# A two-layer hybrid block: Hyena filters stored without their norm, and another order of the start

## The chip, the cores and the metric

The kernel runs on one core of a Trainium2 chip. The metric is the device time of one execution in microseconds (us). The core has five engines with a queue of instructions each: TensorE (PE, with the loading of weights shown apart as PEld), VectorE (DVE), ScalarE (ACT), GpSimd (POOL) and SyncE (SP). Most DMAs of this kernel are issued by SP.

## The reference, cut to what matters

Two layers; in each, a modulated RMS norm feeds one input projection shared by four mixers (a gated recurrence, differential attention, a convolution module and Hyena), then an output projection and a mixture-of-experts FFN. 1024 latent tokens run in both layers, 256 context tokens in the first alone. The shift and scale of the norms are the modulation, `silu(c) @ w_ada + b_ada`, once for `c` and once for `c_ctx`. The change concerns the modulation and the filters of Hyena:

```python
def hyena_filters(L, w_f1, b_f1, freq, w_f2, b_f2, w_f3, decay):
    ...
    f = jnp.sin(freq * (feats @ w_f1 + b_f1))
    f = jnp.sin(freq * (f @ w_f2 + b_f2))
    h = (f @ w_f3) * jnp.exp(-t_unit[:, None] * jnp.abs(decay))
    h = h.astype(jnp.float32).reshape(L, HYENA_ORDER, 2, W_D)
    energy = jnp.sum(jnp.square(h[:, :, 0]), 0) + jnp.sum(jnp.square(h[1:, :, 1]), 0)
    return h * lax.rsqrt(energy + EPS)[None, :, None, :]
...
def hyena_mixer(pd, filt, conv_w, conv_b, h_bias):
    u = dwconv(pd, conv_w, conv_b, (HYENA_SHORT // 2, HYENA_SHORT // 2))
    v, x1, x2 = jnp.split(u, HYENA_ORDER + 1, -1)
    z = v
    for o, gate in enumerate((x1, x2)):
        z = gate * long_conv_bidir(z, filt[:, o, 0], filt[:, o, 1], h_bias[o])
    return z
```

`long_conv_bidir` is a convolution through Fourier transforms plus `z * bias`. There are three sets of filters, none of which depends on `x`: 1024 taps for the first layer's latent tokens, 256 taps for its context tokens, and 1024 taps for the second layer's latent tokens. Since each gate is multiplied into the result of its filter, channel by channel, a factor of a filter may as well stand in its gate.

## The kernel before, in words

**The three filters.** `run` makes them by three calls of `filters`, whose parts are called by number: 0 is the first layer's long filter, 1 the short one for the context, 2 the second layer's long one. A filter has three steps. *network* (letter `p`) loads its weights and computes two sine layers; the argument of each sine is reduced on DVE in a row of small instructions, the sine itself is on ACT; its result is the tile `fc`. *order* (letter `h`, here called the decays) makes, for each block of 128 positions and each of the two gates, a matmul of `fc` with `w3`, an exponential window `e` on ACT, their product on DVE into `hl` (long) or `hs` (short), its square on ACT, and the sum of squares `acc` on POOL: 16 such windows in a long filter, 4 in the short one. Then come the energy by a matmul with ones (L1615), a square root (L1618), the sum and the difference of the filter's two directions (L1620, L1621), the skip bias put into the first tap, and the reciprocal `rs`. *transform* (letter `d`) makes the Fourier transform as matmuls of tables `tab` (128x1024 each, from DRAM) with butterflies of the filter on DVE and POOL (`f_x`, `f_y`, `f_d`; the short filter goes in without them). Each result of 128x512 is multiplied by `rs` on its way out of PSUM (L1651) and stored to DRAM (`hd`, `hdc`), for the convolutions much later. A long transform has 57 such matmuls in two halves and one for the last frequency, 58 in all; the short one has 10.

**The modulation.** `modulation` (letter `m`) streams `w_ada` through three buffers named `wada`, each load 128x4x256 (512 KB), and multiplies it with `sT`, the Silu of the two vectors: four matmuls per load into four row groups of one PSUM tile `mp`. A group of 16 loads gives 2048 columns; the first layer's groups 0 to 2 are made at the start, the others later. At a group's end four small additions put the bias `bada` on, and four stores write `modd` to DRAM.

**The start.** A list, START, names the order in which `run` writes these steps; `n` stands for the loading of the first layer's parameters (L920), of which four rows are of `modd`, and the first norm with its transposes (L1036), after which the input projection begins (L1065):

```python
START = "p0 p1 p2 h0 m0012 h1 d1 h2 d0 n d2"
```

The framework that builds the kernel takes the steps in that order of preference, and may put an instruction ahead of others where its inputs are expected earlier; what it decides is fixed, and each engine then runs its instructions in that order. A DMA stands in the queue of SP among the others. PSUM tiles of the filters' matmuls are five (`mm`), tables have five buffers, `ht` two.

**The gates.** In each layer `hyena_in` (L1713 on) runs Hyena's short convolution on six blocks of 128 channels: 0 and 1 are `v`, 2 to 5 the two gates. One multiplication with the bias on POOL and two multiply-adds on DVE (L1730) cover latent and context tokens together (1281 columns in the first layer, 1024 in the second).

## Time and profile before

| | |
|---|---|
| time, median of 3 runs | 3575.4 us (3574.82 to 3578.94) |
| time of the profiled execution | 3583.19 us |
| its span in the trace | 3581.3 us |
| mean granted TensorE clock | 0.923 of full speed |
| busy share of PE, PEld, DVE, ACT, POOL | 86%, 58%, 64%, 44%, 20% |

The span is the time between the first and the last instruction of the profiled execution; its own time is 1.9 us longer. The busy shares are means over the whole program; the change touches above all the first 277 us of it, so the stretches of that part say more.

### The profile page before, as it was taken

Reading aid. Unit: us, or ns where it says so; the run is one execution under the profiler, and the core shown is the slowest. Engines: PE = TensorE matmul, PEld = TensorE weight load, DVE = VectorE, ACT = ScalarE, POOL = GpSimd, SP = SyncE. Lnnn points to the kernel's source line nnn. Section 1 sums busy time; section 2 is a strip of 40 time slices with the busy share of each in tenths; the row PEclk is TensorE's granted clock in tenths of the full one; section 3 lists DMA queues with packets and bytes.
Section 4 is the critical chain, followed back from the end, with each engine's and each line's share of the span. In section 5 each row is a group of like instructions: output and inputs, shape, how many; then the busy total and the mean of one; then the engine's idle time right before and its main releaser. Section 6 shows DMA issues by size and latency. Waiting matters only on the chain. (4 is left out here: it accounts for less than half of the span.)

```text
span 3581.3 us, 43827 instructions
## 1 busy us (share of the span) xinstructions
PE 3073.7 (86%) x14952; PEld 2071.0 (58%) x14952; DVE 2274.8 (64%) x3297; ACT 1564.7 (44%) x2537; POOL 722.5 (20%) x579
## 2 busy tenths in 40 slices
PE   5798888997899699999997587799779799899993
PEld 1246665775678354676554465667657655465551
DVE  6674885787768433476543778588876653355626
ACT  4234334772334233455543444377323343344533
POOL 2212451003210111111110435300330111111102
PEclk8899899998999699999999798899899899999996
DMA  5752226215565888987878512311546489988796
GB/s 185 230 192 61 69 90 212 70 39 191 161 210 174 286 305 307 369 292 258 318 254 322 170 40 92 135 57 46 174 145 230 151 287 379 378 283 285 270 349 236
DMA packets 415375, 743.33 MB, mean 208 GB/s; under 512 B 46219, under 2 KB 181240, under 8 KB 415146
## 3 DMA queue, kind: packets, MB, share of 16 engines
q1 hardware_dynamic: 397546, 702.69, 56.6%
q0 software_dynamic: 17600, 37.79, 3.1%
q8 instruction: 119, 1.95, 0.2%
q14 instruction: 110, 0.90, 0.1%
HBM read 656.13 MB, written 105.30 MB: 213 GB/s over the span
## 5 line engine op out<-in xcount | busy, mean ns | idle before, releaser
L679 DVE TENSOR_TENSOR wl<-wr,wh 128x1024 fp32r<-128x1024 f32 (+1 forms) x440 | 516.2, 1203 | 395.8 <-ACT wh L678 382.8
L678 ACT ACTIVATE wh<-wr 128x1024 fp32r<-128x1024 f32 (+1 forms) x440 | 442.1, 1038 | 331.5 <-PE mm L730 192.6
L734 PE MATMUL mm<-wr,xl 128*64 128x512 f32 x1216 | 327.6, 607 | 3.4 <-DVE xl L690 1.6
L1065 PE MATMUL mm<-hh,wih 128*128 128x512 f32 (+1 forms) x752 | 290.6, 387 | 13.8 <-ACT stg L1129 8.3
L1065 PE MATMUL mm<-hh,wil 128*128 128x512 f32 (+1 forms) x752 | 289.4, 386 | 10.5 <-POOL wil L951 9.7
L730 PE MATMUL mm<-wh,xh 128*128 128x512 f32 x704 | 288.7, 411 | 6.8 <-ACT wh L678 6.2
L1065 PE MATMUL mm<-hl,wih 128*128 128x512 f32 (+1 forms) x752 | 289.9, 386 | 1.5 <-DVE hl L951 1.0
L730 PE MATMUL mm<-wl,xh 128*128 128x512 f32 x704 | 278.4, 395 | 3.9 <-DVE wl L679 3.8
L730 PE MATMUL mm<-wh,xl 128*128 128x512 f32 x704 | 277.4, 394 | 0.0
L790 POOL DMA_INDIRECT fd<-ot,ridx x82 | 94.3, 1150 | 843.0 <-ACT ot L786 261.0
L1451 DVE SCALAR_TENSOR_TENSOR cacc<-cu,cw,cacc 128x1295 f32<-128x1295 f32 (+1 forms) x120 | 194.5, 1621 | 1.9
L671 POOL DMA_INDIRECT gb<-h2d,ridx x82 | 98.3, 1199 | 466.9 <-PE tr L698 177.9
L730 PEld LDWEIGHTS mm<-wh,xh 128*128 128x128 f32 x704 | 133.0, 189 | 92.6 <-issue 45.1
L1199 DVE TENSOR_REDUCE m<-A 128x1 f32<-128x1024 f32 x128 | 156.2, 1220 | 44.6 <-PE A L1189 36.6
L951 POOL TENSOR_TENSOR wil<-wir,wih 128x1024 fp32r<-128x1024 f32 x34 | 92.5, 2722 | 431.0 <-ACT wih L948 375.3
L734 PEld LDWEIGHTS mm<-wr,xl 128*64 128x64 f32 x1216 | 95.2, 137 | 141.8 <-issue 124.4
L1065 PEld LDWEIGHTS mm<-hh,wih 128*128 128x128 f32 x752 | 147.0, 196 | 44.9 <-ACT stg L1129 11.9
L1065 PEld LDWEIGHTS mm<-hh,wil 128*128 128x128 f32 x752 | 147.5, 196 | 39.1 <-POOL wil L951 10.9
L1065 PEld LDWEIGHTS mm<-hl,wih 128*128 128x128 f32 x752 | 147.4, 196 | 30.8 <-issue 6.2
L780 PE MATMUL mm<-wr,hl 128*64 128x512 f32 x608 | 154.9, 604 | 0.0
L1244 ACT ACTIVATE wT<-TR 128x512 f32<-128x512 f32 (+1 forms) x200 | 104.9, 524 | 108.2 <-PE TR L1239 99.1
L730 PEld LDWEIGHTS mm<-wl,xh 128*128 128x128 f32 x704 | 133.6, 190 | 30.5 <-DVE wl L679 6.7
(491 smaller groups left out, 6527.4 us busy)
## 6 DMA issues: line engine op xcount, KB each, us to landing
wr<-in_moe_w_gate_dram SPq DMA_DIRECT2D x256, 512.0 KB
wr<-in_moe_w_up_dram SPq DMA_DIRECT2D x256, 512.0 KB
wr<-in_moe_w_down_dram SPq DMA_DIRECT2D x256, 512.0 KB
wada<-in_w_ada_dram SPq DMA_DIRECT2D x48, 512.0 KB
tabc<-in_k_t_c_dram SPq DMA_DIRECT2D x88, 256.0 KB
wir<-in_w_in_dram SPq DMA_DIRECT2D x40, 512.0 KB
wr<-in_w_ada_dram SPq DMA_DIRECT2D x32, 512.0 KB
ks<-qkd SPq DMA_DIRECT2D x16, 640.0 KB
```

Source lines behind the costliest of these rows:

```text
L671: self.K.nc.gpsimd.indirect_dma_start(out=g[s, :D // (1 + h)], out_offset=None, in_=self.h2d[h], in_offset=bass.IndirectOffsetOnAxis(ap=id ...
L678: nc.scalar.activation(hi, src, AF.Copy)
L679: nc.vector.tensor_tensor(lo, src, hi.bitcast(FT), op=OP.subtract)
L730: nc.tensor.matmul(ps[b][w], x(k), y[:, kk], start=(k == 0 and c == 0), stop=(k == 7 and c == 2))
L734: nc.tensor.matmul(ps[b][0][w * 64:(w + 1) * 64], self.XT[n0 + b](k), raw[w][:, kk], start=(k == 0), stop=(k == 7))
L780: nc.tensor.matmul(po[b][0][o * 64:(o + 1) * 64], HT[b][:, k], raw[:, o], start=(k == 0), stop=(k == 3))
L790: s = nc.gpsimd.indirect_dma_start(out=self.fd[h], out_offset=bass.IndirectOffsetOnAxis(ap=ridx[r], axis=0), in_=ot[r], in_offset=None, bo ...
L951: (eng or nc.vector).tensor_tensor(lo, src, hi.bitcast(FT), op=OP.subtract)
L1065: nc.tensor.matmul(p[:, :n], a[:, k], b[:, k, t0:t0 + n], start=(k == 0 and a is wh and b is hh), stop=(k == 7 and a is wl))
L1199: nc.vector.tensor_reduce(m[:, c, 1:2], A[c], axis=AX.X, op=OP.max, negate=True)
L1244: nc.scalar.activation(o, i_, AF.Copy)
L1451: nc.vector.scalar_tensor_tensor(a, u[:, j:j + N], cw(j), a, op0=OP.mult, op1=OP.add)
```

## The change

It has four parts. First, the list of the start is another. Second, the filters are transformed and stored without the factor `rs`: each result leaves PSUM by a copy on ACT (L1657 after), and the norm's reciprocal, now made by small matmuls in channel layout (`rsc`, 128x4 for a filter), is multiplied into the gates' convolution weights by `gate_taps`. The skip bias is multiplied with the norm itself, as before. Third, `hyena_in` cuts the blocks 2 to 5 of the first layer into a latent and a context piece, since their norms differ. Fourth, the modulation's `sT` is padded to 32 columns, so that a row group of PSUM is written in full, and one addition for the whole tile replaces four. `ones_f` shares its tile with an index table.

```diff
-START = "p0 p1 p2 h0 m0012 h1 d1 h2 d0 n d2"
+START = "p0 h0 p2 m0012 d0 p1 h2 h1 d1 n d2"
...
-            self.sT = self.keep.tile([P, 8, 2], FT, name="sT")
+            self.sT = self.keep.tile([P, 8, 32], FT, name="sT")
+            nc.vector.memset(self.sT, 0.0)
...
+            nc.gpsimd.memset(b, 0.0)
...
-                        nc.tensor.matmul(p[32 * j:32 * j + 2, h:h + 256], self.sT[:, k], t[:, j], start=(k == 0),
+                        nc.tensor.matmul(p[32 * j:32 * j + 32, h:h + 256], self.sT[:, k], t[:, j], start=(k == 0),
                                          stop=(k == 7))
+            nc.vector.tensor_tensor(b, p, b, op=OP.add)
             for j in range(4):
                 o = (g * 4 + j) * 512
-                m = b[32 * j:32 * j + 2]
-                nc.vector.tensor_tensor(m, p[32 * j:32 * j + 2], m, op=OP.add)
-                nc.sync.dma_start(self.modd[l, :, o:o + 512], m)
+                nc.sync.dma_start(self.modd[l, :, o:o + 512], b[32 * j:32 * j + 2])
...
-            pe = self.psum_mm()
+            pe, pc = self.psum_mm(), self.psum_mm()
             for o in range(2):
                 for d in range(2):
-                    nc.tensor.matmul(pe[:, o * 256:(o + 1) * 256], self.ones_f, acc[:, o, d * 256:(d + 1) * 256],
-                                     start=(d == 0), stop=(d == 1))
-            rs = wd.tile([P, 512], FT, name="rs", bufs=3)
-            nc.scalar.activation(rs, pe, AF.Sqrt, bias=self.eps[:, 0:1])
+                    nc.tensor.matmul(pe[0:1, o * 256:(o + 1) * 256], self.ones_f[:, 0:1],
+                                     acc[:, o, d * 256:(d + 1) * 256], start=(d == 0), stop=(d == 1))
+                for h2 in range(2):
+                    for d in range(2):
+                        nc.tensor.matmul(pc[:, o * 2 + h2:o * 2 + h2 + 1],
+                                         acc[:, o, d * 256 + h2 * P:d * 256 + (h2 + 1) * P], self.ones_f[:, 0:1],
+                                         start=(d == 0), stop=(d == 1))
+            rs = w.tile([P, 512], FT, name="sq", bufs=SB)[0:1]
+            nc.scalar.activation(rs, pe[0:1], AF.Sqrt, bias=self.eps[0:1, 0:1])
+            nc.scalar.activation(rsc, pc[:, 0:4], AF.Sqrt, bias=self.eps[:, 0:1])
+            v.reciprocal(rsc, rsc)
...
-            v.reciprocal(rs, rs)
-            st["h"] = h, rs
+            v.tensor_tensor(rs, self.hbias[32 * l:32 * l + 1], rs, op=OP.mult)
+            v.tensor_tensor(h[0:1, 0, 0], h[0:1, 0, 0], rs, op=OP.add)
+            st["h"] = h
...
-                        v.tensor_tensor(t[:, q], dft(tab, lists[q], A), rs, op=OP.mult)
+                        nc.scalar.activation(t[:, q], dft(tab, lists[q], A), AF.Copy)
...
+    def gate_taps(self, w, n):
...
+        v = self.nc.vector
+        cw = w.tile([P, 3, 4], FT, name="gtap", bufs=2)
+        k = self.col["d_conv_w"]
+        v.tensor_tensor(cw, self.pp[:, k:k + 18].rearrange("p (j b) -> p j b", j=3)[:, :, 2:6],
+                        self.rsc[:, n, None, :].to_broadcast([P, 3, 4]), op=OP.mult)
+        cb = w.tile([P, 4], FT, name="gbias", bufs=2)
+        k = self.col["d_conv_b"]
+        v.tensor_tensor(cb, self.pp[:, k + 2:k + 6], self.rsc[:, n], op=OP.mult)
+        return cw, cb
...
+        if b < 2:
+            parts = [(0, N, lambda j: self.pc("d_conv_w", j * 6 + b), self.pc("d_conv_b", b))]
         else:
-            nc.gpsimd.tensor_scalar(u, x[:, 0:N], self.pc("d_conv_w", b), self.pc("d_conv_b", b), op0=OP.mult,
-                                    op1=OP.add)
-        for j in (1, 2):
-            (nc.gpsimd if HIN[j] else v).scalar_tensor_tensor(u, x[:, j:j + N], self.pc("d_conv_w", j * 6 + b), u, op0=OP.mult, op1=OP.add)
+            parts = [(o, n, lambda j, cw=cw: cw[:, j, b - 2:b - 1], cb[:, b - 2:b - 1])
+                     for (o, n), (cw, cb) in zip(((0, TL), (TL + 1, TC)), taps)]
+        for o, n, cw, cb in parts:
+            nc.gpsimd.tensor_scalar(u[:, o:o + n], x[:, o:o + n], cw(0), cb, op0=OP.mult, op1=OP.add)
+            for j in (1, 2):
+                v.scalar_tensor_tensor(u[:, o:o + n], x[:, o + j:o + j + n], cw(j), u[:, o:o + n], op0=OP.mult,
+                                       op1=OP.add)
```

How the new list moves instructions is seen in the order of each engine's queue. First TensorE at the end of the modulation's stream, before. `mp` is the modulation's tile, `acc` the sum of squares of the second long filter, `f_x` and `f_y` the first filter's butterflies.

```order
L1599 MATMUL mm<-w_238,fc 128x512 x2
L979 MATMUL mp<-wada,sT 2x256 x16
L1615 MATMUL mm<-acc,ones_f 128x256 x3
L979 MATMUL mp<-wada,sT 2x256 x4
L1615 MATMUL mm<-acc,ones_f 128x256
L1634 MATMUL mm<-f_x,tab 128x512
L979 MATMUL mp<-wada,sT 2x256 x4
L1634 MATMUL mm<-f_x,tab 128x512
L979 MATMUL mp<-wada,sT 2x256 x4
L1634 MATMUL mm<-f_x,tab 128x512
L979 MATMUL mp<-wada,sT 2x256 x4
L1634 MATMUL mm<-f_x,tab 128x512
```

After, at the end of the stream (the row of 64 is the third group's 16 loads):

```order
L981 MATMUL mp<-wada,sT 32x256 x4
L1640 MATMUL mm<-f_x,tab 128x512
L981 MATMUL mp<-wada,sT 32x256 x4
L1640 MATMUL mm<-f_d,tab 128x512
L1640 MATMUL mm<-f_x,tab 128x512
L981 MATMUL mp<-wada,sT 32x256 x4
L1640 MATMUL mm<-f_d,tab 128x512
L981 MATMUL mp<-wada,sT 32x256 x64
L1640 MATMUL mm<-f_x,tab 128x512
L1640 MATMUL mm<-f_y,tab 128x512
```

The first layer's transform, of which eight matmuls stood in the stream before, now has 22 in it, all in its second group; its third group is one piece, and the remaining 36 stand behind it.

Next SP's queue from the last loads of the stream on, before (`hdc` is the short filter's spectrum, `hd_109` that of the first layer's long one):

```order
L985 DMA modd<-bada 2x512 x4
L976 DMA wada<-in_w_ada_dram 128x4x256 x13
L969 DMA bada<-in_b_ada_dram 2x512 x4
L985 DMA modd<-bada 2x512 x4
L976 DMA wada<-in_w_ada_dram 128x4x256 x16
L1654 DMA hdc<-ht 128x2x512
L1659 DMA hdc<-ht_823 128x512
L1654 DMA hdc<-ht 128x2x512
L1664 DMA tab<-in_k_t_l_dram 128x1024 x2
L985 DMA modd<-bada 2x512 x4
```

And after (`hd_108` is the first layer's long spectrum, `w_890` a weight of the short filter's network):

```order
L986 DMA modd<-bada 2x512 x4
L978 DMA wada<-in_w_ada_dram 128x4x256 x15
L1660 DMA hd_108<-ht 128x2x512
L1665 DMA hd_108<-ht_745 128x512
L1660 DMA hd_108<-ht 128x2x512
L986 DMA modd<-bada 2x512 x4
L1660 DMA hd_108<-ht 128x2x512
L1670 DMA tab<-in_k_t_l_dram 128x1024 x5
L1541 DMA w_890<-in_d_w_f_dram 33x64
L1552 DMA w_892<-in_d_w_f_dram 64x64
```

The short transform's stores and two tables stood behind the last 16 loads; now the stores of the first layer's spectrum and of `modd` stand there, and the five tables for the rest of its transform behind them. The loads of parameters and tokens for the first norm, which stood ahead of the last store of the first transform, now stand, all but one, behind the last store of the short one.

Last, TensorE where the first layer's long transform ends, before (`f_x` and `f_y` here are of the first layer; L929 transposes the parameters; the next row is the second layer's transform):

```order
L1634 MATMUL mm<-f_x,tab 128x512
L1634 MATMUL mm<-f_y,tab 128x512
L1634 MATMUL mm<-f_x,tab 128x512
L1634 MATMUL mm<-f_y,tab 128x512
L929 MATMUL mm<-ident,hfull 128x126
L1634 MATMUL mm<-f_x,tab 128x512 x2
L930 MATMUL mm<-ident,hfull 128x40
L1634 MATMUL mm<-f_x,tab 128x512 x2
L1634 MATMUL mm<-f_y,tab 128x512 x2
```

And after (`w_890` and `w_892` belong to the short filter's network, `w_343` to the second long filter's decays, `w_893` to the short one's):

```order
L1640 MATMUL mm<-f_y,tab 128x512
L1572 MATMUL mm<-tab,w_890 64x256
L1574 MATMUL mm<-fa,w_892 64x256
L1600 MATMUL mm<-w_343,fc 128x512 x16
L1616 MATMUL mm<-acc,ones_f 1x256 x2
L1620 MATMUL mm<-ones_f,acc 128x1 x4
L1616 MATMUL mm<-acc,ones_f 1x256 x2
L1620 MATMUL mm<-ones_f,acc 128x1 x4
L1600 MATMUL mm<-w_893,fc 128x512 x4
```

The short network, the decays of the second layer's long filter and of the short one, all under the modulation's stream before, now stand behind the last matmul of the first layer's transform, ahead of the short transform and of the second layer's.

## Rows read from the trace of the kernel before

**Rows 1.** Stretches: us, busy us (records) of PE, PEld, DVE, ACT, POOL; clock; DMA.

```profile
169.00:212.00 43.00, 43.00 (x103) 19.00 (x101) 29.46 (x33) 0.23 (x1) 0.00 (x0) 1.00 0.54 187
212.00:277.00 65.00, 61.09 (x194) 27.59 (x193) 51.13 (x85) 34.53 (x68) 15.38 (x10) 1.00 0.56 191
```

**Rows 2.** Timeline of TensorE (start, us, engine, line, operation, count [idle before]).

```profile
218.78 0.65 PE L1036 MATMUL mm<-ident,xn 128*128 128x128 f32 x4
...
267.72 0.41 PE L1036 MATMUL mm<-ident,xn 128*128 128x128 f32 x2
...
277.24 0.80 PE L1065 MATMUL mm<-hh,wih 128*128 128x512 f32 x1
```

**Rows 3.** The same timeline in the modulation's stream.

```profile
100.86 1.04 PE L979 MATMUL mp<-wada,sT 128*2 128x256 f32 x16
103.88 0.61 PE L979 MATMUL mp<-wada,sT 128*2 128x256 f32 x8 [1.97 <-DMA wada<-in_w_ada_dram]
...
119.60 0.61 PE L979 MATMUL mp<-wada,sT 128*2 128x256 f32 x8
...
148.57 0.61 PE L979 MATMUL mp<-wada,sT 128*2 128x256 f32 x8
...
158.60 0.61 PE L979 MATMUL mp<-wada,sT 128*2 128x256 f32 x8 [0.50 <-DMA wada<-in_w_ada_dram]
```

**Rows 4.** Timeline of ACT and POOL: the first filter.

```profile
21.58 0.63 ACT L1522 ACTIVATE fc<-e 128x512 f32<-128x512 f32 x1 [3.33 <-DVE e L1521]
...
45.65 0.72 ACT L1590 ACTIVATE e<-dec,tu 128x512 f32<-128x512 f32 x1
...
58.91 10.51 POOL L1611 TENSOR_TENSOR acc<-acc,sq 128x512 f32<-128x512 f32 x5 [0.83 <-ACT sq L1610]
```

**Rows 5.** Timeline of TensorE at the start of the first transforms.

```profile
163.10 2.05 PE L1634 MATMUL mm<-f_x,tab 128*128 128x512 f32 x2 [3.89 <-DMA tab<-in_k_t_l_dram]
...
173.65 1.02 PE L1634 MATMUL mm<-f_d,tab 128*128 128x512 f32 x2
174.51 1.02 PE L1634 MATMUL mm<-f_x,tab 128*128 128x512 f32 x2
```

**Rows 6.** Timeline of SP's DMA issues, and the first reader of `xin`.

```profile
155.58 2.46 SPq L1664 DMA_DIRECT2D tab<-in_k_t_l_dram  x2
159.98 2.38 SPq L985 DMA_DIRECT2D modd<-bada  x4
...
207.97 0.84 SPq L2024 DMA_DIRECT2D xin<-in_x_dram  x2
...
211.77 1.06 ACT L1019 ACTIVATE xn<-xin 128x1024 f32<-128x1024 f32 x1 [61.23 <-DMA xin<-in_x_dram]
```

**Rows 7.** Timeline of DVE and ACT: the short filter's sine.

```profile
25.47 0.53 DVE L1511 TENSOR_SCALAR e<-mm,fb 64x256 f32<-64x256 f32 x1 [1.74 <-PE mm L1573]
...
28.35 0.42 ACT L1522 ACTIVATE fc<-e 64x256 f32<-64x256 f32 x1 [4.08 <-DVE e L1521]
```

**Rows 8.** Timelines of POOL, DVE and ACT: the decays.

```profile
89.77 7.70 POOL L1611 TENSOR_TENSOR acc<-acc,sq 128x512 f32<-128x512 f32 x2 [20.35 <-ACT sq L1610]
128.18 17.31 POOL L1611 TENSOR_TENSOR acc<-acc,sq 128x512 f32<-128x512 f32 x14 [30.70 <-ACT sq L1610]
...
123.77 1.28 DVE L1602 TENSOR_TENSOR hl<-mm,e 128x512 f32<-128x512 f32 x2
...
151.34 4.42 DVE L1621 SCALAR_TENSOR_TENSOR hl<-hl 128x4096 f32<-128x4096 f32 x1
...
149.85 0.69 ACT L1618 ACTIVATE rs<-mm,eps 128x512 f32<-128x512 f32 x1 [4.84 <-PE mm L1615]
```

**Rows 9.** Groups by line: busy us, mean ns; then durations of one line.

```profile
L1651 DVE TENSOR_TENSOR ht<-mm,rs 128x512 f32<-128x512 f32 x36 | 24.5, 684 | 13.8 <-PE mm L1634 13.8
...
L1626 DVE RECIPROCAL rs<-rs 128x512 f32<-128x512 f32 x3 | 10.0, 3337 | 0.0
...
L1730 DVE SCALAR_TENSOR_TENSOR hu<-hx,pp,hu x24: 1267/1548/2586, 841.0 to 2588.2; 128x1281 f32<-128x1281 f32 x12, 128x1024 f32<-128x1024 f32 x12
```

More of the change, by code (lines that the diff above doesn't have):

```diff
@@ L283, in moe_consts @@
     iota(K.ecol, [[0, P]], 0, 1)
-    d = c.tile([P, P], FT, name="tri_d")
+    K.ones_f = d = c.tile([P, P], FT, name="ones_f")
     iota(d, [[1, P]], 0, -1)
@@ L962, in modulation @@
                                                                ap=[[1, P], [P, 8]]))
-            nc.scalar.activation(self.sT, self.sT, AF.Silu)
+            nc.scalar.activation(self.sT[:, :, 0:2], self.sT[:, :, 0:2], AF.Silu)
         for g in gs:
@@ L1522, in sin_layer, with filters @@
         nc.scalar.activation(out, a, AF.Sin)
-    def filters(self, l, L, hd, wd, w, wh):
+    def filters(self, l, L, hd, wd, w, wh, rsc):
         nc, I = self.nc, self.I
@@ L1611, in order @@
                     nc.gpsimd.tensor_tensor(acc[:, o], acc[:, o], sq, op=OP.add)
-            pe = self.psum_mm()
+            pe, pc = self.psum_mm(), self.psum_mm()
             for o in range(2):
                 for d in range(2):
-                    nc.tensor.matmul(pe[:, o * 256:(o + 1) * 256], self.ones_f, acc[:, o, d * 256:(d + 1) * 256],
-                                     start=(d == 0), stop=(d == 1))
-            rs = wd.tile([P, 512], FT, name="rs", bufs=3)
-            nc.scalar.activation(rs, pe, AF.Sqrt, bias=self.eps[:, 0:1])
+                    nc.tensor.matmul(pe[0:1, o * 256:(o + 1) * 256], self.ones_f[:, 0:1],
[9 more added lines that the diff above has]
+            v.reciprocal(rsc, rsc)
             v.tensor_tensor(h[:, :, 0], h[:, :, 0], h[:, :, 1], op=OP.add)
             v.scalar_tensor_tensor(h[:, :, 1], h[:, :, 1], -2.0, h[:, :, 0], op0=OP.mult, op1=OP.add)
-            bias = w.tile([P, 512], FT, name="sq", bufs=SB)[0:1]
-            v.tensor_tensor(bias, self.hbias[32 * l:32 * l + 1], rs[0:1], op=OP.mult)
-            v.tensor_tensor(h[0:1, 0, 0], h[0:1, 0, 0], bias, op=OP.add)
-            v.reciprocal(rs, rs)
-            st["h"] = h, rs
+            v.tensor_tensor(rs, self.hbias[32 * l:32 * l + 1], rs, op=OP.mult)
+            v.tensor_tensor(h[0:1, 0, 0], h[0:1, 0, 0], rs, op=OP.add)
+            st["h"] = h
         def transform():
-            h, rs = st["h"]
+            h = st["h"]
             def dft(tab, lst, A):
@@ L1723, in hyena_in @@
         u = w.tile([P, N], FT, name="hu", bufs=2)
-        if HIN[0]:
-            nc.scalar.activation(u, x[:, 0:N], AF.Identity, scale=self.pc("d_conv_w", b), bias=self.pc("d_conv_b", b))
-        else:
-            nc.gpsimd.tensor_scalar(u, x[:, 0:N], self.pc("d_conv_w", b), self.pc("d_conv_b", b), op0=OP.mult,
-                                    op1=OP.add)
-        for j in (1, 2):
-            (nc.gpsimd if HIN[j] else v).scalar_tensor_tensor(u, x[:, j:j + N], self.pc("d_conv_w", j * 6 + b), u, op0=OP.mult, op1=OP.add)
+        if b < 2:
+            parts = [(0, N, lambda j: self.pc("d_conv_w", j * 6 + b), self.pc("d_conv_b", b))]
+        else:
+            parts = [(o, n, lambda j, cw=cw: cw[:, j, b - 2:b - 1], cb[:, b - 2:b - 1])
[5 more added lines that the diff above has]
+                                       op1=OP.add)
         nq = ut.shape[1]
@@ L2118, in run @@
             wf = self.pool(cm, "fl", side="right")
-            parts = [self.filters(0, TL, self.hd[0], wd, wf, wf), self.filters(0, TC, self.hdc, wd, wf, wf),
-                     self.filters(1, TL, self.hd[1], wd, wf, wd)]
+            self.rsc = self.keep.tile([P, 3, 4], FT, name="rsc")
+            parts = [self.filters(0, TL, self.hd[0], wd, wf, wf, self.rsc[:, 0]),
+                     self.filters(0, TC, self.hdc, wd, wf, wf, self.rsc[:, 1]),
+                     self.filters(1, TL, self.hd[1], wd, wf, wd, self.rsc[:, 2])]
             self.pm = self.pool(c, "fl_ps", FPS, space=PSUM)
@@ L2167, in run @@
                     w = self.pool(c2, "xy")
+                    taps = [self.gate_taps(hc, n) for n in ((0, 1) if ctx_out else (2,))]
                     for b in range(2):
-                        self.hyena_in(l, hc, b, ut, ctx_out)
+                        self.hyena_in(l, hc, b, ut, ctx_out, taps)
                     next(hy)
@@ L2172, in run @@
                     for b in range(2, 6):
-                        self.hyena_in(l, hc, b, ut, ctx_out)
+                        self.hyena_in(l, hc, b, ut, ctx_out, taps)
                     self.conformer(l, w, ctx_out)
@@ L2261 @@
 POOLP = (2,)
-HIN, HP = (0, 0, 0), "ac"
+HP = "ac"
 CHAIN = (0, 1)
```

5 lines of the change are left out of this document (2 added, 3 removed).

## The prediction

> **What bounds the kernel now.** I read the stretch table of the start first, since all edits but the gates' convolution and the later modulations lie before the first input projection. In it the reader is to see that TensorE, at its full clock, has no idle time from 169 to 212 us (the transforms of the first layer's filters, `d0`) and little from 212 to 277 us (the second layer's, `d2`, with the first norm between them) [rows 1]. The first projection matmul stands at 277.24 us [rows 2]: what moves this moment moves everything behind it, since the order on every engine is nearly the same from there on. So the forecast is a sum for this one moment.
>
> Then the timeline of TensorE. Until 159.2 us it works through the weights of the modulation, 48 loads of 512 KB in three groups of 16, three buffers ahead. Between 103.88 and 119.60 us eight loads took 1.97 us each, between 148.57 and 158.60 us six took 1.67 us each; several of these steps wait for the DMA [rows 3]. Under this stream lie, at no cost, the decays of both long filters and the whole short filter (`h0`, `h1`, `d1`, `h2`). Only `d0` and `d2` come after it. TensorE takes matmuls in the written order: the short filter's energy held it up to 100.86 us, and then two loads that had long landed went by in one piece, x16 in 1.04 us [rows 3].
>
> **The change part by part.** I go through the new START and add up when the first projection can begin. Small edits are priced at the end.
>
> *Stream earlier.* `fc` of the first filter is ready at 21.58 + 0.63 = 22.2 us [rows 4]. Until now its decays waited for the other two filters' networks, and the fourth window's exponential stood at 45.65 us. Now ACT has between the two only three loads of a function table, one exponential (0.72 us [rows 4]), an absolute value, the Silu and a square, some 6.4 us by the same instructions of the timeline before; so it stands near 28.6 us, 17 us earlier. The last add of the energy, 58.91 + 10.51 = 69.42 us on POOL [rows 4], moves to 52.4 us, and the order puts the energy's matmuls ahead of the sixth load's. With 1.3 us for them and 2 us for the second filter's first layer the stream restarts at 55.7 us, 5 loads done and 3 landed. Group 1: 2.5 us for the landed ones, 8 more at 1.67 to 1.97 us (14.5): 72.7 us. Group 2 now has 22 of `d0`'s 58 matmuls between its last 14 loads. Its first four tables are loaded ahead of them. One of these matmuls is two records and takes 0.86 us at full clock (from 173.65 to 174.51 us [rows 5]); four modulation matmuls take 0.61 us; so a load costs 0.61 + 22/14 x 0.86 = 1.96 us on TensorE, as much as the DMA. 72.7 + 0.7 (bias) + 4 (two landed loads, one sine layer's matmuls) + 27.4 = 104.8 us. Group 3: 2 us until its accumulator is free, 2.5 us, 13 loads at 1.67 to 1.97 us (23.6): **133 us** instead of 159.2. Bounds: 127 us with the fast rate throughout; 152 us if `d0`'s 22 run at half clock (1.7 us each, as the first three did after 163.10 us: two records in 2.05 us instead of 1.02 [rows 5]).
>
> *A new wait.* On SP the next five tables of `d0` stand behind the last 15 weight loads, two stores and the group's four `modd` stores. So after 133 us TensorE has nothing to do until a table has come: 0.7 us for the add, 2.4 us for the stores (159.98 us), 0.8 us for a store and the issue, and the landing. For that the rows give 3 us (`xin`, issued by 208.81 us, its reader at 211.77) as the low end and 7.5 us (table issued at 155.58 us, used at 163.10) as the high one [rows 5, 6]. I take 8 us in all, of 7 to 11.
> [...]
>
> *`d0`'s rest*: 36 x 0.86 = 31 us, and 3 us for the half clock after the wait, as before (163.10 us on [rows 5]): 34 us. Only behind these 36 does the order let in the short filter's network and, behind it, the second layer's decays.
>
> *The short network, now bare*: 2.9 us of sine work on DVE and 0.42 us on ACT, twice (25.47 and 28.35 us [rows 7]), and two small matmuls: 8 us. Before, it lay beside the other networks.
>
> *`h2`, now bare*: first product at 123.77 us, POOL's last add ended at 128.18 + 17.31 = 145.49 us: 21.7 us, paced by ACT (an exponential and a square per window) [rows 8]. TensorE has 16 matmuls to do in this time and nothing else.
>
> *From there to the short transforms, now bare*: energy and root 5.1 us (to 149.85 + 0.69 = 150.54 us); the odd half of the filter 4.4 us [rows 8]; POOL's two adds for `h1` 2.5 us (17.31/14 = 1.24 us each at `h2`'s pace; two took 7.7 us beside DVE's work [rows 8]); energy and root again 4.5 us. Between these stand short DVE and ACT instructions: four products of `h1` at 0.64 us (1.28 for two [rows 8]) and a square, 3.7 us, and two biases with a share of the sums and differences of the filters' halves, 3.9 us. Sum 24.1 us. Bounds: 19 us without company, 31 us with the slow adds.
>
> *`d1`*: 10 x 0.86 us and 2.6 us for the clock: 11 us, also out in the open now.
>
> *`d2` and the norm.* 58 x 0.86 = 50 us. The norm's inputs are issued behind `d1`'s last store, so its first transposes come only after 21 matmuls of `d2` (before: from 218.78 us, at its start). 50 of the 80 transposes fit between the others, about 9 us with their waits; 30 stand behind the last one. A group of 16 took from 267.72 us to the end of the stage, 277.24 us less some 2.5 us [rows 2]: 7 us; nearly two groups and the squares between them are 15 us. Sum 74 us, and 1.5 us to the first projection.
>
> Total: 133 + 8 + 34 + 8 + 21.7 + 24.1 + 11 + 74 + 1.5 = **315.3 us** instead of 277.2: **+38 us**.
>
> *Small edits.* The filters' copy out of PSUM goes from DVE (36 of 0.684 us) to ACT, and three reciprocals of 3.34 us shrink to 4 columns [rows 9]. ACT did next to nothing from 169 to 212 us (0.23 us of 43 [rows 1]), and DVE was not what `d0` and `d2` waited for: nothing gained; if ACT were late, each copy would hold one of five PSUM tiles, at most 0.7 us a piece. Where DVE is on the path (bias after `h2`), the lost reciprocal stood behind the bias' forerunner, and I have left it out of the 24.1 us already. The wider `sT` leaves the four products of a load in their four column groups; one add for four at a group's end saves 2 us on DVE twice, inside the stream. In the gates four blocks of the first layer are cut in two pieces: 8 more DVE instructions, each between 1.548 - 1.267 = 0.28 us (no more than the columns) and 1.27 us (a whole long one), less 0.28 us [rows 9]: 0 to 8 us, I take 1 because the stage has idle DVE time, and set the saved adds of the later modulations against it: 0.
>
> The profiled execution took 3583.2 us, 7.8 us over the runs' median of 3575.4; I add the difference to the median: 3575.4 + 38 = **3613 us**.
>
> **Rivals.** *A (smaller loss).* What I took for work was company: the stream at 1.67 us throughout (127 us), the two chains at their bare lengths (19 us for 24, 6 us for 8), the norm's tail half as long, table there after 7 us. Sum 315.3 - 6 - 5 - 2 - 8 - 1 = 293: +16 us, 3591. For it: `h1` and `h2` in the trace share DVE with butterflies. Against: the longest pieces (windows, matmuls) are own work.
>
> *B (not slower).* `d0` and `h2` really run beside each other, as the change's words have it: TensorE takes the decays' matmuls while it waits for the table, and fills their gaps with `d0`. Then the 34 us and the 8 us vanish under the 54 us of network and decays: 315.3 - 42 = 273, -4 us, 3571. It decides where the second layer's first decay matmul stands against the last of `d0`. The order puts all 36 ahead, and the two loads that went by together at 100.86 us [rows 3] show that a ready matmul does not overtake a waiting one.
> [...]
>
> *C (larger loss).* `d0`'s matmuls inside group 2 run at half clock and hold the stream: 152 us instead of 133, and `h1`'s adds are slow (+7): +64 us, 3639. For it: from 163.10 us on three such matmuls took 5.2 us. Against: TensorE is busy nearly without a gap there.
>
> **How the numbers follow.** Mine 0.70 (3598 to 3630 by the terms' bounds), A 0.12, B 0.08, C 0.10. The predicted time is 3613. The range takes in A and stops short of C's middle: 3588 to 3636. A measurement of this kernel tells 0.2% (7 us) from no change. Slower 0.90 (mine, A with a little off for its lower end, C); B divides between no change and faster: same 0.04, faster 0.06.
>
> **What would show it.** Right: the last modulation matmul near 133 us; a TensorE wait for a table of 5 us or more behind it; 36 transform matmuls in a row; then from about 175 to 231 us a TensorE with little to do, at half clock in part; first projection matmul at 300 to 330 us; about equal lengths from there to the end. Wrong: decay matmuls of the second layer among `d0`'s; a first projection before 285 us; or a different length behind it, above all in the gates' stage.

## The result, and the profile after

| | before | after |
|---|---|---|
| time, median | 3575.3 us | 3638.5 us (3633.2 to 3641.1, 4 runs) |
| ratio, 95% interval | | 1.0175 (1.0163 to 1.0188) |
| time of the profiled execution | 3583.2 us | 3641.1 us |
| first projection matmul | 277.2 us [rows 2] | 348.4 us |

The change costs 63 us. The forecast was +38 us and a range that ended at 3636. The sign and the mechanism were right, the size was not. In the profile the first projection comes 71.1 us later and the span is 57.9 us longer, so 13.2 us came back behind it. Of these, 5.3 us are only how the two profiled executions stand to their medians (7.8 us over it before, 2.5 us over it after). By the first layer's FFN (first `tr<-rPM,rcb`, at 1290.6 us before and 1358.1 after) only 3.7 us had come back. The rest lies behind it, where single profiled executions differ by more, so that the other 8 us are a gain is not shown.

The stretch table after, cut at the steps of the forecast (columns as in [rows 1]): the rest of the modulation's first group from where its stream restarts, its second and third group, the wait for a table, the rest of `d0`, the short network, `h2`, the chain up to the short transform, `d1`, `d2`, and the norm's tail.

```profile
57.80:78.10 20.30, 10.95 (x90) 2.36 (x88) 14.90 (x16) 1.94 (x3) 0.00 (x0) 0.58 0.80 251
78.10:115.60 37.50, 34.09 (x175) 10.03 (x175) 14.81 (x17) 3.37 (x6) 0.52 (x1) 0.91 0.72 224
115.60:150.30 34.70, 17.38 (x130) 3.34 (x130) 2.96 (x3) 0.00 (x0) 0.00 (x0) 0.59 0.82 258
150.30:158.30 8.00, 0.00 (x0) 0.00 (x1) 0.69 (x1) 1.08 (x2) 0.00 (x0) 0.50 0.74 218
158.30:191.80 33.50, 33.47 (x73) 14.58 (x73) 6.61 (x8) 6.32 (x10) 0.00 (x0) 0.93 0.61 185
191.80:199.30 7.50, 4.11 (x14) 1.70 (x14) 5.26 (x15) 3.28 (x5) 0.00 (x0) 0.86 0.62 210
199.30:223.00 23.70, 14.27 (x29) 6.00 (x27) 13.18 (x20) 23.11 (x37) 17.23 (x14) 0.64 0.00 1
223.00:258.20 35.20, 20.49 (x54) 10.63 (x52) 22.43 (x22) 8.52 (x12) 9.20 (x3) 0.50 0.00 0
258.20:268.80 10.60, 10.57 (x21) 4.70 (x22) 3.11 (x4) 2.38 (x4) 0.00 (x0) 0.82 0.42 126
268.80:328.30 59.50, 57.33 (x171) 26.29 (x169) 31.83 (x50) 31.14 (x61) 7.99 (x6) 1.00 0.59 201
328.30:348.40 20.10, 8.09 (x32) 3.65 (x30) 8.00 (x23) 15.07 (x28) 4.98 (x14) 0.64 0.45 160
```

The reader is to see two kinds of rows. In the transforms TensorE has almost no idle time, as in [rows 1]. From 191.8 to 258.2 us it works 38.9 of 66.4 us and the DMA, from 199.3 us on, does nothing: what lay under the weights' stream now lies alone. Here the granted clock fell to 0.64 and then to 0.50.

The timeline of TensorE after, at the places of the forecast:

```profile
93.02 1.12 PE L1640 MATMUL mm<-f_y,tab 128*128 128x512 f32 x2
94.08 0.64 PE L981 MATMUL mp<-wada,sT 128*32 128x256 f32 x8
...
121.22 0.64 PE L981 MATMUL mp<-wada,sT 128*32 128x256 f32 x8 [4.02 <-DMA wada<-in_w_ada_dram]
...
128.47 1.08 PE L981 MATMUL mp<-wada,sT 128*32 128x256 f32 x8 [1.11 <-DMA wada<-in_w_ada_dram]
130.51 1.08 PE L981 MATMUL mp<-wada,sT 128*32 128x256 f32 x8 [0.96 <-DMA wada<-in_w_ada_dram]
...
149.19 1.08 PE L981 MATMUL mp<-wada,sT 128*32 128x256 f32 x8 [1.73 <-DMA wada<-in_w_ada_dram]
...
158.33 2.05 PE L1640 MATMUL mm<-f_x,tab 128*128 128x512 f32 x2 [8.06 <-DMA tab<-in_k_t_l_dram]
...
221.86 1.86 PE L1616 MATMUL mm<-acc,ones_f 128*1 128x256 f32 x4 [6.37 <-POOL acc L1612]
223.65 1.87 PE L1620 MATMUL mm<-ones_f,acc 128*128 128x1 f32 x8
...
247.96 1.86 PE L1616 MATMUL mm<-acc,ones_f 128*1 128x256 f32 x4 [11.73 <-POOL acc L1612]
...
338.91 1.26 PE L1037 MATMUL mm<-ident,xn 128*128 128x128 f32 x4 [4.19 <-DVE xn L1026]
...
348.36 0.79 PE L1066 MATMUL mm<-hh,wih 128*128 128x512 f32 x1 [1.60 <-ACT wih L947]
```

The two loads at 128.47 and 130.51 us are 2.04 us apart, each waited for; the last 15 of the third group are 2.00 us apart on average (121.22 to 149.19 us). The table wait is 8.06 us. SP's timeline shows what stands ahead of the third group's loads and of the tables:

```profile
116.37 1.13 SPq L986 DMA_DIRECT2D modd<-bada  x4
117.60 8.72 SPq L978 DMA_DIRECT2D wada<-in_w_ada_dram  x6
...
151.11 1.15 SPq L986 DMA_DIRECT2D modd<-bada  x4
152.36 0.38 SPq L1660 DMA_DIRECT2D hd<-ht  x1
152.78 3.01 SPq L1670 DMA_DIRECT2D tab<-in_k_t_l_dram  x5
```

The short filter's energy waits 11.7 us for POOL's additions. Below stand the row of POOL's timeline for both additions, their durations (shortest, middle and longest in ns), and the first and last of six DVE instructions that ran one after the other from 239.90 us on:

```profile
239.96 9.17 POOL L1612 TENSOR_TENSOR acc<-acc,sq 128x512 f32<-128x512 f32 x2 [16.93 <-ACT sq L1611]
L1612 POOL TENSOR_TENSOR acc<-acc,sq x2: 1257/4603/7949, 240.0 to 247.9; 128x512 f32<-128x512 f32 x2
...
239.90 1.20 DVE L1689 TENSOR_TENSOR f_y<-hl 128x1024 f32<-128x1024 f32 x1
...
245.57 1.21 DVE L1698 TENSOR_TENSOR f_d<-hl 128x1024 f32<-128x1024 f32 x1
```

The two additions were not equally slow. The first began just after the first of the six butterflies and sums and took 7.95 us: it ended 1.1 us after the last of them. The second, with DVE idle, took 1.26 us. In [rows 8] POOL's pace was 1.24 us an addition beside DVE's products, and two took 7.7 us beside other work of DVE.

So the long addition goes with the six instructions on DVE, 7.95 us beside them and 1.26 us behind them; what makes it long is not shown.

### The profile page after: what moved, and what is told of

Its sections match the earlier page's. It is cut to its first block, busy times and chain, and to the rows that moved or that the text cites. A ratio compares the mean times of both kernels' runs of the same rounds, so it can differ in the third digit from the quotient of the medians.

```text
span 3639.2 us, 43955 instructions
## 1 busy us (share of the span) xinstructions
PE 3101.0 (85%) x15000; PEld 2088.3 (57%) x15000; DVE 2234.7 (61%) x3255; ACT 1591.4 (44%) x2583; POOL 728.0 (20%) x589
## 3 DMA queue, kind: packets, MB, share of 16 engines
q1 hardware_dynamic: 397546, 702.69, 55.7%
q8 instruction: 120, 1.97, 0.2%
```

## The experiments

Ratios are to the kernel before, measured beside each; the medians of before were 3575.5 to 3578.9 us there, and its single times lay up to 31 us apart, so small differences are read from the intervals. Where a stretch is named, it is read from the run's profile, which is one execution. The modulation's stream ended 5 us apart in two of them with the same code there (159.2 us before, 164.5 in the run with split gates), and from the first `tr<-rPM,rcb` to the end, four with the same code there took 2277 to 2291 us.

**The list and the rest, apart.** First the changed kernel with the old list:

```diff
-START = "p0 h0 p2 m0012 d0 p1 h2 h1 d1 n d2"
+START = "p0 p1 p2 h0 m0012 h1 d1 h2 d0 n d2"
```

> The changed kernel with the old START list; all its other edits stay. Theory (the list alone makes the loss; the edits of the arithmetic are free or better): first projection matmul within 6 us of 277 us, and the time 3560 to 3577 us, since the stretch behind the first projection was 13 us shorter in the changed kernel's profiled execution than before and some 5 us of that is how the two profiled executions stand to their medians. Rival (the unnormalised filters cost something themselves: ACT's copies, 16 small energy matmuls a filter, the split gates): first projection later than 285 us or a time over 3585 us.

Measured: 1.0030 (1.0014 to 1.0045), first projection at 302.4 us. The rival's part is there: 25 us were lost at the start (14 in the stream, which ended at 173.2 us; 4 more in the table wait; 7 from there on), and some 14 us came back later. In sum the other edits cost some 11 us (5 to 16), not nothing.

Then the kernel before with `START = "p0 h0 p2 m0012 d0 p1 h2 h1 d1 n d2"` alone:

> The kernel before with the new START list alone. Theory (the list makes the loss): first projection matmul at 340 to 355 us, time 3640 to 3652 us, a little above the changed kernel, which gains some microseconds behind the first projection. Rival (the order and the copies on ACT or the small energy matmuls make the loss together): first projection below 330 us, time below 3628 us.

Measured: 1.0153 (1.0127 to 1.0179), 55 us; first projection at 336.2 us. The list makes nearly nine tenths of the loss. Both the time and the first projection are below the theory's bands and above the rival's: the other edits do not gain but lose a little in sum, as the run before this one shows.

**The stream.** Four weight buffers in the changed kernel (it no longer holds the `rs` tiles):

```diff
-                        t = w.tile([P, 4, 256], FT, name="wada", bufs=3)
+                        t = w.tile([P, 4, 256], FT, name="wada", bufs=4)
```

> The changed kernel with four buffers instead of three for the modulation's weights. Its loads came 2.0 us apart with TensorE waiting for each of them. Theory A (three buffers in a round trip of 6 us set the pace): 1.55 to 1.7 us a load, stream's end near 138 instead of 150 us, time 10 to 13 us lower, 3626 us. Theory B (the transfers' rate sets it): spacing and end of the stream within 3 us of the changed kernel, time 3633 to 3641 us.

Measured: 3624.6 us, 1.0139 (1.0113 to 1.0165), stream's end at 132.8 us. The first, two neighbouring and the last load of its third group:

```profile
107.12 1.08 PE L981 MATMUL mp<-wada,sT 128*32 128x256 f32 x8 [6.30 <-DMA wada<-in_w_ada_dram]
...
123.16 1.08 PE L981 MATMUL mp<-wada,sT 128*32 128x256 f32 x8 [0.38 <-DMA wada<-in_w_ada_dram]
124.63 1.08 PE L981 MATMUL mp<-wada,sT 128*32 128x256 f32 x8 [0.39 <-DMA wada<-in_w_ada_dram]
...
131.67 1.08 PE L981 MATMUL mp<-wada,sT 128*32 128x256 f32 x8 [1.19 <-DMA wada<-in_w_ada_dram]
```

The 16 loads come 1.64 us apart ((131.67 - 107.12)/15; many 1.47), where in the changed kernel the last 15 of the group came 2.00 us apart (121.22 to 149.19 us), both with TensorE at half clock (1.08 us for a load's matmuls, 0.64 us at full clock as in the row at 94.08 us): three buffers in a round trip set the pace, not the transfers. But the time of this run does not price the buffer alone, since the order moved too. Only 6 of `d0`'s matmuls stayed in the stream (the trace of before shows 6 there too, not eight), and the 52 behind it took 47.3 us instead of 33.5 for 36: of the 17.5 us at the stream's end 13.8 are work that moved. A table now stood ahead of the `modd` stores, and the wait for it fell from 8.1 to 2.1 us. So the first projection came 9.6 us earlier (338.8 us), some 6 of them from the shorter wait.

The tables on POOL's DMA queue instead of SP's:

```diff
-        self.nc.sync.dma_start(t, self.I["k_t_" + sfx][k])
+        (self.nc.gpsimd if name == "tab" and bufs == FTABS and sfx == "l" else self.nc.sync).dma_start(
+            t, self.I["k_t_" + sfx][k])
```

> The changed kernel with the long filters' tables loaded from POOL's DMA queue instead of SP's, so that they don't stand behind the weight loads. The framework then puts 32 matmuls of the first layer's transform into the stream instead of 22. Theory (the 8 us wait behind the stream is the queue of SP): the wait shrinks to under 2 us; the stream ends up to 5 us later with the ten matmuls more, which are missing behind it (8.6 us); first projection 9 to 13 us earlier, at 335 to 340 us, time near 3627 us. Rival (the tables share the transfers' rate with the weights): the stream ends 10 us later or more, and first projection within 4 us of 348.

Measured: 1.0178 (1.0161 to 1.0194), first projection at 346.8 us: no gain, and the rival is right. The wait behind the stream is gone, but the stream's last load comes 12 us later:

```profile
161.26 1.08 PE L981 MATMUL mp<-wada,sT 128*32 128x256 f32 x8 [1.96 <-DMA wada<-in_w_ada_dram]
163.27 3.66 PE L1640 MATMUL mm<-f_y,tab 128*128 128x512 f32 x4 [0.92 <-ACT ht L1657]
```

The queue made the wait, as predicted, but to move the tables to another queue was worth nothing here: their transfers and the ten matmuls more are paid in the stream.

**The bare chain.** Network and second decays back under the stream, by `START = "p0 h0 p2 p1 m0012 h2 d0 h1 d1 n d2"`:

> The changed kernel with START = p0 h0 p2 p1 m0012 h2 d0 h1 d1 n d2: the short network and the second layer's decays go back under the modulation's stream, the first layer's transform stays split as it is (22 matmuls in the stream, 36 behind it). Theory (the bare chain of network, decays, energy behind the transform is the largest part of the loss): stream's end at 150 to 158 us, some 16 us of short decays and 11 us of short transform behind the first layer's transform instead of 67 and 11, first projection at 298 to 308 us, time near 3593 us. Rival (the decays would hold the stream by as much as they cost in the open): stream's end later than 175 us, time over 3615 us.

Measured: 1.0057 (1.0040 to 1.0074), 3594.9 us, first projection at 312.0 us. The chain behind `d0` is 15.3 us instead of 66.4; the stream ends at 168.1 instead of 150.3, later than the theory's 158, and the first projection is 4 us behind its band. So 44 us of the 63 come back. The chain in the open is the main loss; putting it under the stream costs a third of it there.

The short filter's additions on DVE:

```diff
-                    nc.gpsimd.tensor_tensor(acc[:, o], acc[:, o], sq, op=OP.add)
+                    (nc.gpsimd if long else v).tensor_tensor(acc[:, o], acc[:, o], sq, op=OP.add)
```

> The changed kernel with the two additions of the short filter's squares on DVE instead of POOL. On POOL they took 9.2 us beside the butterflies on DVE, and TensorE waited 11.7 us for them. Theory (that wait is on the path): 6 to 9 us gone between the short decays and the short transform, first projection at 339 to 343 us, time near 3631 us. Rival (DVE is busy with the butterflies in this time and the additions queue behind them): first projection above 345 us, time within 4 us of the changed kernel's 3638.5.

Measured: 1.0150 (1.0130 to 1.0171), 3629.7 us, 9 us less, with the first projection at 343.3 us, 5 us earlier, though the stream of this execution, which the edit does not touch, ended 2.6 us later. The second energy now starts 4.5 us after TensorE's last matmul instead of 11.7:

```profile
242.67 1.87 PE L1616 MATMUL mm<-acc,ones_f 128*1 128x256 f32 x4 [4.52 <-DVE acc L1612]
```

The reciprocal norms late: the eight small matmuls, the root and the reciprocal go from `order` into a step of their own.

```diff
-            pe, pc = self.psum_mm(), self.psum_mm()
+            pe = self.psum_mm()
...
+        def norms():
+            acc, pc = st["acc"], self.psum_mm()
...
-START = "p0 h0 p2 m0012 d0 p1 h2 h1 d1 n d2"
+START = "p0 h0 p2 m0012 d0 r0 p1 h2 h1 d1 r2 r1 n d2"
```

> The changed kernel with the reciprocal norms (the eight small matmuls of a filter, their root and their reciprocal) made later: the first filter's behind its transform, the other two's behind the short transform. The energy itself stays where it is. Theory (the small matmuls at half clock, 3.7 us a filter, hold the chain, since TensorE takes them ahead of the decays' and the transform's matmuls): 2 us less in the stream, two times 3.7 us less in the chain, 3 to 6 us paid behind the short transform; first projection at 341 to 345 us, time 3631 to 3635 us. Rival (they lie beside ACT's root and DVE's sums anyway): first projection above 347 us, time above 3636 us.

Measured: 1.0167 (1.0151 to 1.0183), first projection at 353.6 us: the rival is right. In TensorE's timeline of that run the energy's second half waits for POOL in the place where the small matmuls had stood, and they cost 3.6 us behind `d1`:

```profile
223.73 1.86 PE L1616 MATMUL mm<-acc,ones_f 128*1 128x256 f32 x4 [5.27 <-POOL acc L1612]
229.13 1.87 PE L1616 MATMUL mm<-acc,ones_f 128*1 128x256 f32 x4 [3.54 <-POOL acc L1612]
...
268.75 3.63 PE L1633 MATMUL mm<-ones_f,acc 128*128 128x1 f32 x32
```

The small matmuls added to the kernel before (result unused):

```diff
+                for h2 in range(2):
+                    for d in range(2):
+                        nc.tensor.matmul(pc[:, o * 2 + h2:o * 2 + h2 + 1],
+                                         acc[:, o, d * 256 + h2 * P:d * 256 + (h2 + 1) * P], self.ones_f[:, 0:1],
+                                         start=(d == 0), stop=(d == 1))
```

> The kernel before with the small energy matmuls of the change added (eight 128x1 matmuls for each filter, their root and their reciprocal, whose result is not used) and nothing taken away. With the old list and the changed arithmetic the modulation's stream ended at 173 instead of 159 us. Theory (the small matmuls stand in the stream ahead of the weights' matmuls, 3.7 us a filter at half clock, and root, wait and lower clock come on top): stream's end at 168 to 174 us, first projection at 286 to 294 us, time 9 to 15 us above the kernel before. Rival (the stream is longer for the padded columns, the one addition at a group's end or the copies): stream's end below 164 us, time within 6 us of the kernel before.

Measured: 1.0006 (0.9989 to 1.0024). In the profile the stream ends at 177.4 us and the first projection stands at 296.3, even beyond the theory's bands; the time is in the rival's. The stream is 18 us longer, well over the 5 us by which unchanged ones differ, so the small matmuls do lengthen it when all decays lie under it (the runs with and without late norms below say the same). Why the time does not follow stays open: the profiled execution was the slowest of its ten, is still 19.9 us late at the first `tr<-rPM,rcb`, and has 6.7 us of it left at its end.

**The norm and the copies.** The copies out of PSUM on DVE in the changed kernel:

```diff
-                        nc.scalar.activation(t[:, q], dft(tab, lists[q], A), AF.Copy)
+                        v.tensor_copy(t[:, q], dft(tab, lists[q], A))
...
-                        nc.scalar.activation(t2[0:1], nyq[0:1], AF.Copy)
+                        v.tensor_copy(t2[0:1], nyq[0:1])
```

> The changed kernel with the filters' copies out of PSUM on DVE (as the multiplication was) instead of ACT. In the order on TensorE 16 instead of 30 of the norm's transposes then stand behind the last transform matmul. Theory (ACT's queue, with copies, squares and the norm's evacuations, makes the norm late): the tail between the last transform matmul and the first projection falls from 20 us to about 12.6, as in the run of the new list alone; first projection at 339 to 343 us, time near 3631 us. Rival (the norm is late for its inputs, wherever the copies are): tail of 18 us or more, time above 3635 us.

Measured: 1.0143 (1.0119 to 1.0167), 3631.1 us, but the first projection at 348.6 us. The tail fell to 12.2 us as expected; 5 us had been lost by the start of `d2`, and `d2` itself took 3 us more with the transposes in it. Of the 5 us, 3 were lost at the stream's end. Half of the theory: the copies on ACT make the tail, but the tail is not all gain. The same with the old list:

> The changed kernel with the old START list and the copies on DVE. With the copies on ACT and the old list the first projection stood at 302.4 us, 25 us later than before: 14 in the modulation's stream, 4 in the table wait behind it, 7 in the second transform and the norm. Theory: only the last 7 to 11 us come back, first projection at 291 to 295 us, time 3571 to 3576 us, no different from the kernel before. Rival (the copies are not what moves the norm): first projection over 299 us, time over 3579 us.

Measured: 1.0006 (0.9990 to 1.0022), first projection at 294.5 us, as expected, with no tail. Copies on ACT, priced at nothing, cost 8 us at the first projection there. As in the run with small matmuls, the first projection is still 17 us later than before while the time is the same.

**The gates.** The kernel before with the blocks 2 to 5 of the first layer in two pieces:

```diff
-            nc.gpsimd.tensor_scalar(u, x[:, 0:N], self.pc("d_conv_w", b), self.pc("d_conv_b", b), op0=OP.mult,
-                                    op1=OP.add)
...
+        for o, n in ((0, N),) if b < 2 or not ctx_out else ((0, TL), (TL + 1, TC)):
+            nc.gpsimd.tensor_scalar(u[:, o:o + n], x[:, o:o + n], self.pc("d_conv_w", b), self.pc("d_conv_b", b),
+                                    op0=OP.mult, op1=OP.add)
```

> The kernel before with one thing of the change: the gates' blocks 2 to 5 of the first layer in a latent and a context piece. In every run with the changed arithmetic the stretch of the first layer's Hyena from its first transform matmul to its last sum was 8 to 10 us shorter than before, and not so with the new list alone. Theory (the split does it: the latent pieces come out of DVE earlier, and TensorE's transposes of the gates wait less for them): the same stretch, 57.2 us before, takes 47 to 50 us, and the first layer's output projection comes 4 to 8 us earlier behind the first projection; time 3568 to 3575 us. Rival (it is the spectra, stored by ACT's copies without a norm, or the order of the queue behind them): stretch of 55 us or more, time within 3 us of the kernel before.

Measured: 0.9984 (0.9970 to 0.9999), 5 us faster, with an interval that all but reaches no change. The durations by line (ns, then first and last start in us) of the kernel before and of this run give the stretch from the first `z_x` to the first `Ysum`, 57.2 and 48.2 us, and the output projection's first matmul on Hyena's context tokens (`yhz`):

```profile
L1774 PE MATMUL mm<-z_x,tabc x128: 379/379/792, 853.6 to 2655.6; 128*128 128x256 f32 x128
L1774 PE MATMUL mm<-Ysum,tabc x96: 379/379/796, 910.8 to 2679.2; 128*128 128x256 f32 x96
L1944 PE MATMUL mm<-woh,yhz x56: 392/399/400, 1056.1 to 2807.8; 128*128 128x512 f32 x56
...
L1773 PE MATMUL mm<-z_x,tabc x128: 379/379/683, 859.2 to 2657.8; 128*128 128x256 f32 x128
L1773 PE MATMUL mm<-Ysum,tabc x96: 379/379/634, 907.4 to 2681.8; 128*128 128x256 f32 x96
L1943 PE MATMUL mm<-woh,yhz x56: 392/399/400, 1060.4 to 2810.5; 128*128 128x512 f32 x56
```

So the split takes 9 us out of its stretch. Counted from the first projection (277.2 and 281.4 us), 3.4 us are left at the output projection's first matmul, under the 4 to 8 expected, and none at `yhz` (778.9 and 779.0 us). There TensorE had waited longer for DVE in this run, and its granted clock fell; the rows of before come first:

```profile
1045.58 1.10 PE L1912 MATMUL tr<-ident,h 128*128 128x128 f32 x8 [1.73 <-DVE h L1957]
1050.00:1056.00 6.00, 6.00 (x28) 4.97 (x27) 5.41 (x23) 3.87 (x7) 0.00 (x0) 1.00 0.93 320
...
1046.62 1.10 PE L1911 MATMUL tr<-ident,h 128*128 128x128 f32 x8 [2.62 <-DVE h L1956]
1051.50:1055.50 4.00, 4.00 (x11) 3.03 (x11) 3.48 (x20) 3.45 (x6) 0.00 (x0) 0.50 0.89 289
```

The changed kernel waits 2.72 us at this place and keeps 3.7 us by the first `tr<-rPM,rcb`; in the fastest version below, where TensorE does not wait there, 8.5 us are kept. By the medians the run is faster, but the profile has no place for it: what of the 9 us the split brings to the time is not shown.

**A faster version.** All decays and the short transform under the stream (`START = "p0 h0 p2 p1 m0012 h1 d1 r0 h2 d0 r1 r2 n d2"`), with late norms, four buffers and the additions on DVE, copies on ACT:

> The changed arithmetic with START = p0 h0 p2 p1 m0012 h1 d1 r0 h2 d0 r1 r2 n d2 (r: the reciprocal norms, late), four weight buffers and the short filter's additions on DVE: all decays and the short transform under the stream, 56 of the first layer's transform matmuls behind it. Theory (order, small energy matmuls and three buffers are what the changed kernel loses): stream's end at 140 to 150 us, table wait under 3 us, first projection at 264 to 276 us, time 3555 to 3569 us, faster than the kernel before. Rival (TensorE at half clock under the stream is the bound as soon as all decays lie there): stream's end over 162 us, first projection over 282 us, time over 3575 us.

Measured: 0.9995 (0.9983 to 1.0008). The stream ended at 146.6 us as expected, but the first projection stood at 287.0 us, with a tail of 20 us for the norm, and the time is no better than before. The same without the late norms (`START = "p0 h0 p2 p1 m0012 h1 d1 h2 d0 n d2"`):

> The changed arithmetic, copies on ACT, with START = p0 h0 p2 p1 m0012 h1 d1 h2 d0 n d2, four weight buffers and the short filter's additions on DVE (the run with all decays under the stream, without the late norms). The late norms kept the memory of the filters' work tiles busy until the first transform was done, and the first norm's tiles lie in the same memory; without them the norm's first transposes may come some 10 us sooner. Theory: 14 transposes behind the last transform matmul instead of 30, tail 11 us instead of 20, first projection at 274 to 280 us, time 3562 to 3570 us. Rival: no change against that run, 287 us and 3577 us.

Measured: 0.9962 (0.9947 to 0.9978), 3563.0 us, first projection at 280.5 us, tail 11.5 us. The stream ended at 156.4 us, 10 later than with late norms: the small matmuls are back in it. And with the copies on DVE besides:

> As the run with the copies on ACT beside it, but with the copies on DVE. Theory: no transpose behind the last transform matmuls, tail near 0 as in the kernel before, first projection at 262 to 270 us, time 3552 to 3562 us, faster than the kernel before by 0.4 to 0.6%. Rival (DVE, which has the butterflies, becomes what the transforms wait for): the two transforms take as much longer as the tail gets shorter, first projection over 273 us.

Measured: 0.9951 (0.9934 to 0.9969), 3560.3 us, the fastest. TensorE goes from the last transform matmul into the projection without a gap:

```profile
273.83 1.02 PE L1640 MATMUL mm<-f_y,tab 128*128 128x512 f32 x2
274.29 0.80 PE L1066 MATMUL mm<-hh,wih 128*128 128x512 f32 x1
```

Its first projection is only 3 us earlier than in [rows 2] and 4 us later than forecast for it, past the rival's bound of 273 us as well: of the 11.5 us of the tail, some 6 went into longer transforms. The time is 18 us lower. In the profiles 8.5 us of that lie between the first projection and the first `tr<-rPM,rcb`, where the split gates are; the rest lies behind, where single executions differ by as much, and I can't place it.

## Why the prediction was wrong in size

Step by step, against its sum of 315.3 us (measured 348.4):

- *Stream earlier*, 133 us: 150.3 (+17.3), the largest miss, and in each of its steps: the restart at 57.8 us instead of 55.7, the first group's rest 20.3 us instead of 17.0, the second group 37.5 instead of 32.1, the third 34.7 instead of 28.2. Three things were wrong. The rates of 1.67 to 1.97 us a load [rows 3] were read where TensorE had other work and its full clock; where the loads stood alone, in the first and third groups (granted clock 0.58 and 0.59), they came 2.0 to 2.2 us apart. I had taken the old rate for a property of the transfers; with four buffers they came 1.64 us apart at half clock. In the third group one load had landed at its start, not three: the other 15 stand on SP behind the second group's `modd` stores (116.37 us), and the second was there only at 121.22 us. And in the second group, with TensorE at its full clock (1.00 from 84.7 to 115.5 us), the 14 loads and 22 matmuls took 30.8 us instead of 27.4: between two loads such a matmul took up to 1.06 us (93.02 to 94.08), where 0.86 us had been read from a row of them. The low bound of 127 us does not follow from the sum either, since the 14 loads cost 1.96 us on TensorE at any rate of the DMA; with the fast rate elsewhere it gives 130.
- *A new wait*, 8 us: 8.06, in part by luck: the `modd` stores took 1.15 us instead of 2.4, and the first table came 5.5 us after its issue began (152.78 to 158.33 us), where 8 us had left some 4.5. In the run with POOL's queue the wait went and nothing was gained; in the run with four buffers 6 us of it went and counted.
- *`d0`'s rest* 34 us: 33.5. *The short network* 8 us: 7.5. *`d1`* 11 us: 10.6. All right.
- *`h2`* 21.7 us: 23.7. Paced by ACT, as said.
- *The chain to the short transforms*, 24.1 us, at most 31: 35.2 (+11.1). The additions were taken at 1.24 us each, POOL's pace beside DVE's products; they took 9.2 us, beyond the slow row (7.7) [rows 8], the first alone 7.95 us, beside six DVE instructions in a row. The run with the additions on DVE got 9 us of time back. The energies took 7.2 us each at the 0.50 clock, half of it the new small matmuls, which the sum left out; the run with late norms shows that to move them away gains nothing.
- *`d2` and the norm*, 75.5 us with the step to the projection: 79.6 (+4.1). The 30 transposes stood behind, as read from the order; the tail was 20 us, not 15.
- *Small edits*, 0: wrong on both sides. The wider `sT` made the four products of a load 0.64 us long (94.08 us) instead of 0.61 [rows 3]. Copies on ACT made the norm late; splitting the gates, priced as a cost of 0 to 8 us, takes 9 us out of its stretch, of which 3.7 are left in the changed kernel. All edits but the list cost 11 us (5 to 16) in the run with the old list.
- *About equal lengths behind the first projection*: the sum missed by 33 us there and the time by only 25, since 8 us came back behind it, which the forecast did not have. That is luck.

Rival B did not come: as the order said, 36 transform matmuls ran in a row before the first decay (196.4 us). Rival A's shorter terms appeared nowhere. Rival C's time was close (3639), its mechanism was not: the 22 matmuls inside the second group ran at a granted clock of 0.91. Its other half, slow additions, was right. One flaw runs through the misses: times of a piece of work were read in one company and used for it in another, where it met a lower clock, a busier DVE or loads between its matmuls.

## What to carry to other kernels

Work that moves from under a stream of loads into the open may cost more there than its rows in company say: here TensorE's granted clock was 0.50 in the bare chain, and one addition on POOL took 7.95 us beside DVE's butterflies, 1.26 us behind them. Before a stream is taken for bound by its rate, count its buffers: with one more, the same loads came 1.64 instead of 2.00 us apart. And look at what stands ahead of the loads on their queue: 15 of the third group's stood behind four small stores. A wait that is seen on a queue may be worth nothing when the transfers behind it are then paid in the stream.

## What was not expected of the hardware

An addition of 128x512 on POOL took 7.95 us beside six DVE butterflies and sums in a row, ending 1.1 us after the last, and 1.24 us beside DVE's products [rows 8]; on DVE itself the two took 0.69 and 0.68 us. The last 3.4 us of what the split gates saved were gone after one longer wait of TensorE (2.62 us instead of 1.73), behind which its granted clock was 0.50 instead of 1.00. Single executions of the unchanged kernel, measured beside the experiments, spread from 3561 to 3596 us, more than several of the effects here.
